# Hybrid state-space, pooling and stick-breaking block on one core: ScalarE empties the value products a pair at a time, output projection in 512-column blocks, other banks and earlier token sums ahead of the first seven-product block

## The chip, the cores and the metric

The kernel runs on one core of a Trainium2 chip. The metric is the device time of one launch in microseconds (us). PE is TensorE, with PEld its weight loads; DVE is VectorE, ACT is ScalarE, POOL is GpSimd, SP is SyncE, which here issues DMAs. The core has an SBUF of 128 partitions, in which tiles live, and a PSUM of eight banks, each 128 partitions x 512 fp32 columns, into which PE writes.

## The reference

One layer, sequence S = 1024, width D = 1024, all in float32. The heart of it is:

```python
h = rms_norm(x, norm_w)
z, xbc, dt_raw, pool_u, pool_gate, qkv, sb_gate, merge = split(h @ w_in)
y_ssm  = mamba2_branch(z, xbc, dt_raw, ...) @ w_proj_ssm     # causal conv, chunked scan, gate, norm
y_pool = pool_branch(pool_u, pool_gate, ...) @ w_proj_pool   # trailing means over 2, 4, 8, 16
y_sb   = stick_breaking_branch(qkv, sb_gate) @ w_proj_sb     # below
g = sigmoid(merge)                                           # three gates per channel
merged = g0 * y_ssm + g1 * y_pool + g2 * y_sb
return rms_norm(x + merged @ w_out, final_norm_w)
```

The attention has 16 heads of 64 and no softmax. For query t and key s < t, with z = q·k/8, its weight is sigmoid(z_s) times the product of sigmoid(−z) over the keys between s and t; a scan from the right computes that product. The result o = att @ v is multiplied by silu(gate).

## The kernel before

**Numbers.** Each fp32 operand is held as two fp32r parts, hi and lo, and a product is three matmuls, hi·hi, hi·lo and lo·hi. A contraction over 1024 is so 8 k-tiles x 3 = 24 matmuls into one bank. `gemm_b` (L396) has weights stationary and 512 tokens moving, `gemm_a` (L405) tokens stationary and 256 weight columns moving. Weights come in halves of 512 KB: `load_half` (L102) issues the DMA on SP, `split_half` (L110) makes hi on ACT (L128) and lo on DVE (L129) in a ring `wpool` of four halves; `mm()` (L413) hands out a PSUM bank in a fixed rotation, two of the pool `mm` and then `mmx` of the pool `mmx`, counted from `mmb`, and triggers the split of a coming half.

**Stages in the order of the program.**

1. `norm_in` (L548): eight tiles of x, row norms (Square on ACT L567, rsqrt on POOL L545, scale on DVE L573), transposes on PE (L588) into `hT` as hi (ACT) and lo (DVE L592). Constants: `cm` (identity, masks) and `cols` (per-channel vectors).
2. `conv_part` (L705): projection block x0 with its causal convolution, the last z block together with dt (`zd_open` L594 casts its weights, L605 and L606), gate block g0, x1, g1. Between them a table of steps puts the token sums `one`, `two`, `three` (L227 to L255): sums and differences of blocks of `hT`, each cast to hi on ACT (L260) and lo on DVE (L261).
3. Fourteen seven-product blocks (`seven_block` L281). A block of 256 columns x 1024 tokens is done with seven half-size products instead of eight, in four banks x, y, z, v. `seven_prep` (L140) makes the weight sums of a block, s1 to s4 and the hi and lo parts (`lo` is L176), for the first one inside g1's loop; the products are L299, the additions on DVE L309.
4. `attention_part` (L860): 64 units (p, hd, ip): eight pairs of heads, the head of the pair, and four groups of 256 queries. For each unit `stage_qk` (two scores' rows: matmuls L891, sigmoids on ACT L895 and L898, scan on DVE L900, multiplication L901 to `be`), `stage_tr` (transposes on PE L918, hi on ACT L920, lo on DVE L921) and `stage_av` (value products L942). The value products of a unit stand three sub-steps behind its transposes, so the last of them come in the loop of the next unit but one. Between the sub-steps PE is filled with projections for later (`fill`). All value products go to one bank `avs`, columns 0 to 255 for even ip, 256 to 511 for odd; the stationary v carries its hi part in 64 columns and its lo part in the other 64, so the bank's two 64-row halves hold two partial results, and a unit's end adds them: ACT copies one half out (L947), DVE adds the other from PSUM (L948). After an odd ip POOL multiplies by the gate (L950) and SP stores.
5. `ssd_part` (L1104), `pool_part` (L987).
6. `merge_part` (L1279): the three branches' projections and the gates, then the output projection: four blocks of 256 columns x eight token tiles, each 24 matmuls; DVE adds the residual (L1342), ACT squares with a row sum (L1344); in the last block each tile is finished one tile late: sum (L1329), rsqrt on POOL, a multiplication by r and the final weight (L1333), store (L1334).

**What sets the order.** PE's order is written by hand in the whole program; that of DVE, ACT and POOL too in `norm_in` and `conv_part` with the seven-product blocks. In attention and merge a scheduler orders ACT, POOL and DVE by estimated times, but for DVE in the output projection, which is again as written. Each engine then runs its list in order. SP issues DMAs in its list's order.

Of the kernel before, what the change touches and what calls it, by code (L numbers as in the profile page):

```python
# [8 lines left out]
F32 = mybir.dt.float32  # L9
# [34 lines left out]
def block_plan():  # L44
# [30 lines left out]
    for i in range(4):  # L75
        plan.append((("out", i), "w_out", 0, [(256 * i, 256)]))
    return plan
# [6 lines left out]
class Builder:  # L84
# [25 lines left out]
    def split_half(self):  # L110
        nc = self.nc
        n = self.wnext
        if n >= self.limit():
            return
        self.wnext += 1
        raw = self.raw.pop(n)
        if n // 2 == BLK["z", 0]:
            w = self.zd[:, :, 4 * (n % 2) : 4 * (n % 2) + 4, 0:256]
        else:
            w = self.wpool.tile([P, 2, 4, 256], F32R, tag="w", name=f"w{n}")  # L120
        raw = raw.rearrange("p (a b) -> p a b", b=256)
# [426 lines left out]
    def norm_in(self, pool, pps):  # L548

        nc = self.nc  # L550
        xts = []
        for t in range(8):
            xt = pool.tile([P, D], F32, tag="xt", name=f"xt{t}", bufs=8)
            nc.sync.dma_start(out=xt, in_=self.ins["x"][t * P : t * P + P, :])
            xts.append(xt)
            if t == 3:
                consts = self.constants()
                next(consts)
                self.load_half()
# [146 lines left out]
    def conv_part(self):  # L706
        with ExitStack() as ctx:
            ctx.enter_context(self.tc.manual_schedule(engines={mybir.EngineType.PE, mybir.EngineType.DVE, mybir.EngineType.Pool, mybir.EngineType.Activation}))
            pool = self.c_pool = self.sb(ctx, "c_sb", 3, "right")
            plain = ExitStack()  # L710
            self.ps_extra(plain, "c_ps", 3)
            pps = self.ps(plain, "n_ps", 3)

# [11 lines left out]
            for i, _ in enumerate(self.conv_gen(0, pool, norm)):  # L725
                if i == 2:
                    self.zd_open(dpool)
# [3 lines left out]
            one, two, three = self.seven_operands(tpool, dpool)  # L731
            dt = self.dt_part(dpool, {1: (one, 0), 3: (two, 0), 5: (one, 1), 7: (two, 1)})
            next(dt)
            zctx.close()
            self.tt[4] = self.sb(ctx, "t4_sb", 1, "right").tile([P, 2, 4, 512], F32R, name="tt4")
            steps = {8: (three, 0), 24: (three, 1), 48: (one, 2), 72: (three, 2)}
            for i, _ in enumerate(self.g_gen(0)):
# [7 lines left out]
            self.wseven = {}  # L745
            steps = {4: (two, 2), 16: (one, 3), 32: (three, 3), 44: (two, 3)}
            prep = {}
            for i, _ in enumerate(self.g_gen(1)):
                if i in steps:
                    steps[i][0](steps[i][1])  # L750
                if i == 14:
                    self.drain(dt)
                    dctx.close()
                    self.wspool = self.sb(ctx, "ws_sb", 2)
                if i == 50:
                    self.t_flush()
# [99 lines left out]
    def attention_part(self):  # L856
        tc, nc = self.tc, self.nc
        A, V, T, G = nc.scalar, nc.vector, nc.tensor, nc.gpsimd
        with ExitStack() as ctx:
# [64 lines left out]
            def stage_av(u, jc):  # L924
# [19 lines left out]
                if jc == ip:  # L944
                    other = slice(64 - 64 * hd, 128 - 64 * hd)
                    cs = slice(256 * (ip % 2), 256 * (ip % 2) + 256)
                    A.copy(o[rows, cs], ps[other])  # L947
                    V.tensor_tensor(out=o[rows, cs], in0=o[rows, cs], in1=ps[rows], op=ALU.add)  # L948
                    if ip % 2 == 1:
                        G.tensor_tensor(out=o[rows], in0=o[rows], in1=gt[rows], op=ALU.mult)  # L950
                        nc.sync.dma_start(out=self.d_y["sb"][p // 4][rows, p % 4, hs], in_=o[rows])

# [328 lines left out]
    def merge_part(self):  # L1281
        tc, nc = self.tc, self.nc
        A, V, T, G = nc.scalar, nc.vector, nc.tensor, nc.gpsimd
        with ExitStack() as ctx:
            ctx.enter_context(self.bigctx)
            self.ps_extra(ctx, "m_ps", 4)
            with ExitStack() as c2:
                pacc = self.sb(c2, "m_acc", 1, "right")
# [27 lines left out]
            with ExitStack() as c2:  # L1316
# [5 lines left out]
                for t in range(8):  # L1322
                    nc.sync.dma_start(out=res[t], in_=self.ins["x"][t * P : t * P + P, :])
                c2.enter_context(tc.manual_schedule(engines={mybir.EngineType.DVE}))

                def finish(t):
                    ot = pool.tile([P, D], F32, tag="ot", name="ot", bufs=3)
                    ss = pool.tile([P, 1], F32, tag="fss", name="fss", bufs=2)
                    V.tensor_reduce(out=ss, in_=ssq[:, t], axis=mybir.AxisListType.X, op=ALU.add)  # L1329
                    r = self.rstd(pool, ss, D, "f")  # L1330
                    step = D if t < 7 else D // 2
                    for c in range(0, D, step):
                        V.scalar_tensor_tensor(ot[:, c : c + step], res[t][:, c : c + step], r, fw[:, c : c + step], op0=ALU.mult, op1=ALU.mult)  # L1333
                        nc.sync.dma_start(out=self.out[t * P : t * P + P, c : c + step], in_=ot[:, c : c + step])  # L1334

                for b in range(4):
                    w = self.block(("out", b))
                    cs = slice(b * 256, b * 256 + 256)
                    for t in range(8):
                        ps = self.mm()[:, 0:256]  # L1340
                        self.drain(self.gemm_a(ps, w, lambda pt, k, t0, t1: mh[k][:, pt, t0:t1], t))
                        V.tensor_tensor(out=res[t][:, cs], in0=ps, in1=res[t][:, cs], op=ALU.add)  # L1342
                        sq = pool.tile([P, 256], F32, tag="sq", name="sq", bufs=2)
                        A.activation(sq, res[t][:, cs], AF.Square, accum_out=ssq[:, t, b : b + 1])  # L1344
                        if b == 3 and t > 0:
                            finish(t - 1)
                finish(7)


def host_arrays(i):  # L1350
# [7 lines left out]
    for _, src, row, cols in PLAN:  # L1358
        m = np.concatenate([mats[src][row : row + 1024, c : c + n] for c, n in cols], axis=1)
        blocks.append(tiles(m).reshape(P, 2048))  # L1360
# [43 lines left out]
```

## Time and profile before

| quantity | value |
|---|---|
| median of 3 runs | 2077.47 us (2076.37 to 2077.67) |
| the profiled execution, its own time | 2076.43 us |
| its span, first to last instruction | 2074.7 us |
| mean granted PE clock | 0.991 |
| busy: PE, PEld, DVE, ACT, POOL | 98%, 83%, 64%, 46%, 14% of the span |
| chain of work that ended last | PE 78%, DVE 15%, ACT 4% |
| stages | norm, convolution 0 to 155 us; seven-product blocks to 435; attention to 1200; scan, pooling to 1640; merge to 1974; output to 2074.7 |

The chain of the page follows the work that ended last back through what released it; the stage borders are read from the lines of PE's timeline and rounded. PE's list of waits tells, for each kind of instruction, what released it and for how long PE stood idle before.

### The profile page before, as it was taken

The page shows a single profiled execution, that of the slowest core. Times are in us where ns is not written, and L with a number is a line of the kernel's source. Part 1 is how long each engine was busy: PE and PEld are TensorE (multiplying, and loading weights), DVE is VectorE, ACT ScalarE, POOL GpSimd, SP SyncE. Part 2 cuts the span into 40 slices and gives each one's busy share as a digit, 9 for nine tenths or more (in the row PEclk, how much of TensorE's full clock was granted, in tenths as well). Part 3 has the DMA queues.
Part 4 walks back from the last instruction along what each step waited for, and adds up shares of the span by engine and source line. Part 5 has one row for each costly group of instructions (what it writes and reads, how often), then busy time and mean ns, then how long its engine had stood idle before and what let it go on. Part 6 is the DMA issues. An engine that isn't in the chain of part 4 may idle for free.

```text
span 2074.7 us, 29592 instructions
## 1 busy us (share of the span) xinstructions
PE 2026.5 (98%) x11312; PEld 1726.4 (83%) x11312; DVE 1333.1 (64%) x1857; ACT 952.4 (46%) x1953; POOL 292.5 (14%) x412
## 2 busy tenths in 40 slices
PE   8989999999999899999999899999999999999998
PEld 6978878788898788989898888778888788888898
DVE  6687788847767767676668647777657724424333
ACT  4353433335555655455556456667543423323231
POOL 3000000001111111010111124444200002221000
PEclk9999999999999999999999999999999999999999
DMA  5222232341121122112121266666464625433232
GB/s 201 94 95 102 85 119 91 112 155 57 42 72 36 41 78 61 57 56 68 55 72 46 62 201 210 198 201 200 140 202 142 213 92 192 144 115 107 82 132 82
DMA packets 116157, 234.00 MB, mean 113 GB/s; under 512 B 9776, under 2 KB 59696, under 8 KB 116016
## 3 DMA queue, kind: packets, MB, share of 16 engines
q1 hardware_dynamic: 116016, 232.12, 34.4%
q8 instruction: 89, 1.46, 0.3%
q14 instruction: 52, 0.43, 0.1%
HBM read 168.38 MB, written 63.70 MB: 112 GB/s over the span
## 4 chain that ended last, share of the span: by engine, by line
PE 78%; DVE 15%; ACT 4%; issue 3%; DMA 1%; DVEq 0%; POOL 0%; ACTq 0%; SPq 0%; POOLq 0%
PE mm L396 27%; PE mmx L396 14%; PE mm L405 12%; PE mmx L299 4%; DVE om L900 4%; PE mmx L405 4%; PE av L942 3%; DVE acc L358 3%; PE yd L1171 3%; PE tr L918 2%; PE mm L299 1%; PE yo L1174 1%; PE st L1177 1%; DVE be L901 1%; PE z L891 1%
## 5 line engine op out<-in xcount | busy, mean ns | idle before, releaser
L396 PE MATMUL mm<-hT,w 128*128 128x512 f32 x2232 | 584.3, 405 | 1.9 <-DVE hT L592 1.8
L396 PEld LDWEIGHTS mm<-hT,w 128*128 128x128 f32 x2232 | 406.2, 190 | 92.9 <-issue 15.1
L405 PE MATMUL mm<-w,hT 128*128 128x256 f32 x2112 | 287.9, 286 | 2.0 <-issue 1.1
L405 PEld LDWEIGHTS mm<-w,hT 128*128 128x128 f32 x2112 | 265.1, 191 | 3.4 <-ACT qb L835 1.6
L396 PE MATMUL mmx<-x,w 128*128 128x512 f32 x1008 | 230.3, 389 | 0.0
L129 DVE TENSOR_TENSOR w<-raw,w 128x1024 fp32r<-128x1024 f32 x116 | 150.1, 1296 | 113.3 <-ACT w L128 113.2
L396 PEld LDWEIGHTS mmx<-x,w 128*128 128x128 f32 x1008 | 189.3, 188 | 39.2
L900 DVE TENSOR_TENSOR_SCAN om<-om,zero 128x128 f32<-128x128 f32 (+7 forms) x128 | 175.5, 1372 | 61.8 <-ACT om L895 60.9
L920 ACT CAST attT<-tr 128x512 fp32r<-128x512 f32 (+2 forms) x224 | 98.3, 439 | 138.9 <-PE tr L918 86.1
L921 DVE TENSOR_TENSOR attT<-tr,attT 128x512 fp32r<-128x512 f32 (+2 forms) x224 | 111.2, 497 | 67.3 <-ACT attT L920 65.6
L128 ACT CAST w<-raw 128x1024 fp32r<-128x1024 f32 x116 | 121.5, 1050 | 61.2 <-PE mmx L396 27.6
L895 ACT ACTIVATE om<-z 128x128 f32<-128x128 f32 (+2 forms) x192 | 92.7, 496 | 68.0 <-PE z L894 67.1
L396 PE MATMUL mm<-x,w 128*128 128x512 f32 x528 | 122.6, 389 | 0.0
L1300 ACT ACTIVATE gt<-gt 128x1024 f32<-128x1024 f32 x32 | 34.0, 1062 | 185.9 <-DMA gt<-d_gate 185.9
L396 PEld LDWEIGHTS mm<-x,w 128*128 128x128 f32 x528 | 99.1, 188 | 20.6
L396 PE MATMUL mmx<-hT,w 128*128 128x512 f32 x456 | 105.0, 390 | 0.0
L901 DVE TENSOR_TENSOR be<-be,om 128x128 f32<-128x128 f32 (+7 forms) x128 | 98.1, 767 | 10.5
L396 PEld LDWEIGHTS mmx<-hT,w 128*128 128x128 f32 x456 | 85.4, 188 | 17.6
L1148 POOL TENSOR_TENSOR E<-E,cbm 128x1024 f32<-128x1024 f32 x32 | 76.6, 2395 | 160.9 <-issue 104.8
L898 ACT ACTIVATE be<-z 128x128 f32<-128x128 f32 (+2 forms) x192 | 92.5, 500 | 0.1
L918 PE MATMUL tr<-cm,be 128*128 128x128 f32 x576 | 90.3, 274 | 0.5 <-DVE be L901 0.5
L1309 POOL TENSOR_TENSOR acc<-acc,gt 128x512 f32<-128x512 f32 x32 | 45.6, 1426 | 247.0 <-DVE gt L1308 125.9
(250 smaller groups left out, 3255.7 us busy)
## 6 DMA issues: line engine op xcount, KB each, us to landing
raw<-in_wblk SPq DMA_DIRECT2D x148, 512.0 KB, 4.1
E<-d_act SPq DMA_DIRECT2D x32, 512.0 KB, 4.7
gt<-d_gate SPq DMA_DIRECT2D x32, 512.0 KB, 4.0
d_gate<-mg SPq DMA_DIRECT2D x16, 512.0 KB, 3.1
xi<-d_x SPq DMA_DIRECT2D x32, 256.0 KB, 3.2
zs<-d_z SPq DMA_DIRECT2D x32, 256.0 KB, 2.9
d_ssm<-yt SPq DMA_DIRECT2D x32, 256.0 KB, 3.1
xraw<-d_ssm SPq DMA_DIRECT2D x16, 512.0 KB, 6.0
```

Of the source, the lines that this page charges most:

```text
L128: nc.scalar.copy(hi, raw)
L129: nc.vector.tensor_tensor(out=lo, in0=raw, in1=hi.bitcast(F32), op=ALU.subtract)
L299: T.matmul(ps, w[a](i, k), mov[b](j, k), start=first and n == 0, stop=n == 11, skip_group_check=not first)
L396: T.matmul(ps, w(a, k, ct * P, ct * P + P), mov(b, k, half * 512, half * 512 + 512), start=n == 0, stop=n == 23)
L405: T.matmul(ps, sta(a, k, tok * P, tok * P + P), w(b, k, 0, ncol), start=n == 0, stop=n == 23)
L895: A.activation(om[:, c0 : c0 + n], z[:, 0:n], AF.Sigmoid, scale=-0.125)
L898: A.activation(be[:, c0 : c0 + n], z[:, 0:n], AF.Sigmoid, scale=0.125)
L900: V.tensor_tensor_scan(out=rev, data0=rev, data1=self.zero.broadcast_to((P, L)), initial=1.0, op0=ALU.mult, op1=ALU.add)
L901: V.tensor_tensor(out=be[:, 0:L], in0=be[:, 0:L], in1=om[:, 1 : L + 1], op=ALU.mult)
L918: T.transpose(tr[:, c : c + P], b[:, (2 * jc + j) * P : (2 * jc + j + 1) * P], self.ident)
L920: A.copy(at[:, 0, sl], tr[:, sl])
L921: V.tensor_tensor(out=at[:, 1, sl], in0=tr[:, sl], in1=at[:, 0, sl].bitcast(F32), op=ALU.subtract)
```

## The change

Six edits:

- **Value products (L934 on).** The bank is a fresh tile per pair of units (pool `a_av`, one buffer). Only after the odd ip it is emptied: ACT copies all of it to SBUF (`oa`), ACT copies the other head half across to `o`, DVE adds the two from SBUF over 512 columns; multiplication and store as before.
- **Output projection.** Two blocks of 512 columns, each of four halves (two k-tiles x 512 columns), 24 matmuls of 512 columns per token tile; the host lays `w_out` out accordingly. Halves 0, 1, 6 and 7 go to a pool of their own, the triggers by `mm()` are off. The last tile's second block is done in two pieces of 256 columns, its columns multiplied by the final weight ahead of the norm, and at the end DVE scales one half and ACT the other.
- **First seven-product block.** The pool of the norm's banks is opened before the convolution's, and the rotation starts two later (`mmb -= 2`), so a block takes `mmx` four times and the next `mmx` twice and `mm` twice.
- **Token sums.** `one`, `two`, `three` come earlier in the loops of dt, g0 and g1, as do the six steps of the first block's weight sums.
- **Constants.** `cm` and `cols` load after x tile 0 instead of x tile 3.
- **dt.** `zd_open` comes after the second instead of the third step of the first convolution's loop.

```diff
-    for i in range(4):
-        plan.append((("out", i), "w_out", 0, [(256 * i, 256)]))
+    for i in range(4):
+        plan.append((("out", i), "w_out", 512 * (i % 2), [(512 * (i // 2), 512)]))
...
+        elif n - 2 * BLK["out", 0] in (0, 1, 6, 7):
+            w = self.wext.tile([P, 2, 4, 256], F32R, tag="wx", name=f"w{n}")
...
+        consts = self.constants()
         for t in range(8):
+            if t == 1:
+                next(consts)
...
             if t == 3:
-                consts = self.constants()
-                next(consts)
...
+            pps = self.ps(plain, "n_ps", 3)
             self.ps_extra(plain, "c_ps", 3)
-            pps = self.ps(plain, "n_ps", 3)
...
-                if i == 2:
+                if i == 1:
                     self.zd_open(dpool)
...
-            dt = self.dt_part(dpool, {1: (one, 0), 3: (two, 0), 5: (one, 1), 7: (two, 1)})
+            dt = self.dt_part(dpool, {0: (one, 0), 2: (two, 0), 4: (one, 1), 6: (two, 1)})
-            steps = {8: (three, 0), 24: (three, 1), 48: (one, 2), 72: (three, 2)}
+            steps = {2: (three, 0), 18: (three, 1), 36: (one, 2), 60: (three, 2), 84: (two, 2)}
...
-            steps = {4: (two, 2), 16: (one, 3), 32: (three, 3), 44: (two, 3)}
+            steps = {2: (one, 3), 20: (three, 3), 34: (two, 3)}
...
-                if i == 50:
+                if i == 46:
                     self.t_flush()
                     prep = self.seven_prep(BLK[SEVEN[0]])
-                if i > 50 and i % 8 == 0 and prep:
+                if i % 8 == 6 and prep:
                     prep.pop(min(prep))()
...
             self.ps_extra(ctx, "seven_ps", 6)
+            self.mmb -= 2
...
-            avs = self.ps(ctx, "a_av", 1).tile([P, 512], F32, name="av")
+            pav = self.ps(ctx, "a_av", 1)
...
+                    if ip % 2 == 0:
+                        av[0] = pav.tile([P, 512], F32, tag="av", name="av")
-                ps = avs[:, 256 * (ip % 2) : 256 * (ip % 2) + 256]
+                ps = av[0][:, 256 * (ip % 2) : 256 * (ip % 2) + 256]
...
-                if jc == ip:
+                if jc == ip and ip % 2 == 1:
                     other = slice(64 - 64 * hd, 128 - 64 * hd)
-                    cs = slice(256 * (ip % 2), 256 * (ip % 2) + 256)
-                    A.copy(o[rows, cs], ps[other])
-                    V.tensor_tensor(out=o[rows, cs], in0=o[rows, cs], in1=ps[rows], op=ALU.add)
-                    if ip % 2 == 1:
-                        G.tensor_tensor(out=o[rows], in0=o[rows], in1=gt[rows], op=ALU.mult)
+                    oa = pool.tile([P, 512], F32, tag="oa", name="oa", bufs=1)
+                    A.copy(oa, av[0])
+                    A.copy(o[rows], oa[other])
+                    V.tensor_tensor(out=o[rows], in0=o[rows], in1=oa[rows], op=ALU.add)
+                    G.tensor_tensor(out=o[rows], in0=o[rows], in1=gt[rows], op=ALU.mult)
...
-                for b in range(4):
-                    w = self.block(("out", b))
-                    cs = slice(b * 256, b * 256 + 256)
+                def piece(d, t, c0, c1, n):
+                    ps = self.mm()[:, 0 : c1 - c0]
+                    w = lambda part, k, a, b: wd[k // 2][:, part].rearrange("p a b -> p (a b)")[:, 512 * (k % 2) + c0 - 512 * d + a : 512 * (k % 2) + c0 - 512 * d + b]
+                    self.drain(self.gemm_a(ps, w, lambda pt, k, t0, t1: mh[k][:, pt, t0:t1], t, c1 - c0))
+                    r = res[t][:, c0:c1]
+                    V.tensor_tensor(out=r, in0=ps, in1=r, op=ALU.add)
+                    sq = pool.tile([P, 512], F32, tag="sq", name="sq", bufs=2)[:, 0 : c1 - c0]
+                    A.activation(sq, r, AF.Square, accum_out=ssq[:, t, n : n + 1])
+                    if t == 7:
+                        V.tensor_tensor(out=last[:, c0:c1], in0=r, in1=fw[:, c0:c1], op=ALU.mult)
+                for d in range(2):
+                    while self.wnext < first + 4 * d + 4:
+                        self.split_half()
+                    wd = [self.wh.pop(first + 4 * d + i) for i in range(4)]
                     for t in range(8):
-                        ps = self.mm()[:, 0:256]
...
-                        if b == 3 and t > 0:
-                            finish(t - 1)
-                finish(7)
+                        if (d, t) != (1, 7):
+                            piece(d, t, 512 * d, 512 * d + 512, d)
+                        if d == 0 and t in (2, 4):
+                            self.split_half()
+                        if d == 1 and t > 0:
+                            root(t - 1)
+                            if t < 7:
+                                finish(t - 1)
+                piece(1, 7, 512, 768, 1)
...
+                finish(6)
+                piece(1, 7, 768, 1024, 2)
...
+                V.tensor_scalar(last[:, 0:512], last[:, 0:512], r, None, op0=ALU.mult)
+                nc.sync.dma_start(out=self.out[7 * P :, 0:512], in_=last[:, 0:512])
+                A.activation(last[:, 512:D], last[:, 512:D], AF.Copy, scale=r)
+                nc.sync.dma_start(out=self.out[7 * P :, 512:D], in_=last[:, 512:D])
```

Line numbers of the new kernel are two higher from L128 on, four higher in attention and up to seven higher at the end of the value products.

DVE's list where the first pair of units ends its value products (other pairs have the like), before (`om` is the scan, `be` the multiplication, `attT` the lo part of the transposed weights, `o` the add of a unit's end, `va`, `vb` and `zsg` a projection's):

```order
459 L901 TENSOR_TENSOR be<-be,om 128x896
460 L921 TENSOR_TENSOR attT<-tr,attT 128x512
461 L900 SCALAR_TENSOR_TENSOR om<-om,zero 128x1024
462 L948 TENSOR_TENSOR o<-o,av 64x256
463 L901 TENSOR_TENSOR be<-be,om 128x1024
464 L921 TENSOR_TENSOR attT<-tr,attT 128x512
465 L803 TENSOR_TENSOR va_3638<-mm,va_3638 128x2x64
466 L805 TENSOR_TENSOR vb_3639<-mm,vb_3639 128x2x64
467 L921 TENSOR_TENSOR attT<-tr,attT 128x256
468 L808 TENSOR_TENSOR zsg<-zsg,mm 128x256
469 L921 TENSOR_TENSOR attT<-tr,attT 128x128
470 L948 TENSOR_TENSOR o<-o,av 64x256
```

and in the changed kernel at the same place:

```order
459 L905 TENSOR_TENSOR be<-be,om 128x896
460 L925 TENSOR_TENSOR attT<-tr,attT 128x512
461 L904 SCALAR_TENSOR_TENSOR om<-om,zero 128x1024
462 L905 TENSOR_TENSOR be<-be,om 128x1024
463 L925 TENSOR_TENSOR attT<-tr,attT 128x512
464 L807 TENSOR_TENSOR va_3637<-mm,va_3637 128x2x64
465 L809 TENSOR_TENSOR vb_3638<-mm,vb_3638 128x2x64
466 L925 TENSOR_TENSOR attT<-tr,attT 128x256
467 L812 TENSOR_TENSOR zsg<-zsg,mm 128x256
468 L925 TENSOR_TENSOR attT<-tr,attT 128x128
469 L955 TENSOR_TENSOR o<-o,oa 64x512
470 L904 SCALAR_TENSOR_TENSOR om<-om,zero 128x128
```

The first unit's add, which stood behind the 1024-column scan, is gone, and one add of 512 columns from SBUF stands where the second unit's add was, one row earlier.

DVE's list at the end of g1, ahead of the first seven-product block, before (`gsg` is the gate's multiplication from PSUM, `tt` the lo part of a token sum, `s` the weight sums, `w` and `ws` the lo parts of weights, of which the first is that of a11):

```order
152 L787 TENSOR_TENSOR gsg<-gsg,mmx 128x512
153 L261 TENSOR_TENSOR tt_525<-td,tt_525 128x512
154 L179 TENSOR_TENSOR s_1238<-raw_970,raw_1059 128x512
155 L180 TENSOR_TENSOR s_1239<-s_1238,raw_970 128x512
156 L183 TENSOR_TENSOR s_1240<-raw_970 128x512
157 L184 TENSOR_TENSOR s_1241<-raw_1059,s_1239 128x512
158 L787 TENSOR_TENSOR gsg<-gsg,mm 128x512
159 L176 TENSOR_TENSOR w_1235<-raw_970,w_1235 128x4x128
160 L176 TENSOR_TENSOR ws_1237<-raw_1059,ws_1237 128x4x256
161 L176 TENSOR_TENSOR w_1235<-s_1239,w_1235 128x4x128
```

and in the changed kernel:

```order
151 L247 TENSOR_TENSOR td<-td,te 128x512
152 L263 TENSOR_TENSOR tt_525<-td,tt_525 128x512
153 L181 TENSOR_TENSOR s_1229<-raw_977,raw_1066 128x512
154 L182 TENSOR_TENSOR s_1230<-s_1229,raw_977 128x512
155 L791 TENSOR_TENSOR gsg<-gsg,mmx 128x512
156 L185 TENSOR_TENSOR s_1231<-raw_977 128x512
157 L186 TENSOR_TENSOR s_1232<-raw_1066,s_1230 128x512
158 L178 TENSOR_TENSOR w_1226<-raw_977,w_1226 128x4x128
159 L178 TENSOR_TENSOR ws_1228<-raw_1066,ws_1228 128x4x256
160 L791 TENSOR_TENSOR gsg<-gsg,mm 128x512
```

Behind the weight sums only one multiplication from PSUM, of an `mmx` bank, is left ahead of a11's lo part; the last two, of `mm` banks, stand behind it.

PE's list where the last seven-product block gives way to attention's first projection, before:

```order
553 L299 MATMUL mmx<-hT_107,ws_2974 128x512 x3
554 L299 MATMUL mmx<-hT_108,ws_2974 128x512 x3
555 L299 MATMUL mmx<-hT_109,ws_2974 128x512 x3
556 L299 MATMUL mmx<-hT_110,ws_2974 128x512 x3
557 L299 MATMUL mmx<-tt_818,ws_2974 128x512 x12
558 L299 MATMUL mmx<-hT_107,ws_2974 128x512 x3
559 L299 MATMUL mmx<-hT_108,ws_2974 128x512 x3
560 L299 MATMUL mmx<-hT_109,ws_2974 128x512 x3
561 L299 MATMUL mmx<-hT_110,ws_2974 128x512 x3
562 L405 MATMUL mm<-w_3139,hT_103 128x256 x3
```

and in the changed kernel:

```order
553 L301 MATMUL mmx<-hT_107,ws_2974 128x512 x3
554 L301 MATMUL mmx<-hT_108,ws_2974 128x512 x3
555 L301 MATMUL mmx<-hT_109,ws_2974 128x512 x3
556 L301 MATMUL mmx<-hT_110,ws_2974 128x512 x3
557 L301 MATMUL mm<-tt_818,ws_2974 128x512 x12
558 L301 MATMUL mm<-hT_107,ws_2974 128x512 x3
559 L301 MATMUL mm<-hT_108,ws_2974 128x512 x3
560 L301 MATMUL mm<-hT_109,ws_2974 128x512 x3
561 L301 MATMUL mm<-hT_110,ws_2974 128x512 x3
562 L407 MATMUL mm<-w_3139,hT_103 128x256 x3
```

The last products go to banks of the pool `mm` instead of `mmx`, and the projection that follows takes a bank of `mm` as before.

## Rows read from the trace of the kernel before

**Rows 1.** The profile's page, part 1: busy us (share of the span), instructions.

```profile
PE 2026.5 (98%) x11312; PEld 1726.4 (83%) x11312; DVE 1333.1 (64%) x1857; ACT 952.4 (46%) x1953; POOL 292.5 (14%) x412
```

**Rows 2.** The waits of PE, whole run: us in total, times, longest.

```profile
PE av L942 <- DVE o L948: 18.3, 14, 3.0
PE mm L299 <- DVE gsg L787: 5.3, 1, 5.3
PE tp L588 <- DMA cm<-in_cmat: 2.2, 1, 2.2
...
PE mmx L405 <- DVE zd L605: 1.7, 1, 1.7
```

**Rows 3.** One stretch of the run (attention): length, busy us of each engine, PEclk, DMA, GB/s.

```profile
435.00:1200.00 765.00, 742.38 (x4913) 661.70 (x4912) 529.40 (x758) 412.08 (x935) 98.42 (x253) 0.99 0.19 57
```

**Rows 4.** Timeline, 537.2 to 541.2 us: start, duration, engine, operation [idle before it].

```profile
537.91 2.28 DVE L900 TENSOR_TENSOR_SCAN om<-om,zero 128x1024 f32<-128x1024 f32 x1
538.05 0.36 ACT L947 COPY o<-av 64x256 f32<-64x256 f32 x1
...
540.22 0.42 DVE L948 TENSOR_TENSOR o<-o,av 64x256 f32<-64x256 f32 x1
...
540.70 0.80 PE L942 MATMUL av<-attT,vb 128*128 128x256 f32 x2 [2.64 <-DVE o L948]
```

**Rows 5.** Windows, PE alone: length, busy us, granted clock.

```profile
540.46:543.87 3.41, 3.17 (x10) 0.50 0.00 0
...
1182.15:1185.60 3.45, 3.21 (x16) 0.51 0.00 0
144.50:151.30 6.80, 3.64 (x9) 0.50 0.47 156
```

**Rows 6.** Timeline at a pair's end, 547.2 to 549.8 us.

```profile
547.23 0.36 ACT L947 COPY o<-av 64x256 f32<-64x256 f32 x1
...
549.74 0.36 PE L942 MATMUL av<-attT,vb 128*128 128x256 f32 x1
```

**Rows 7.** ACT by line and shape: busy us, mean ns, idle before.

```profile
L1078 ACT COPY mg<-mm 128x512 f32<-128x512 f32 x48 | 27.9, 582 | 41.8 <-PE mm L396 41.7
...
L947 ACT COPY o<-av 64x256 f32<-64x256 f32 x64 | 23.5, 368 | 22.5 <-PE av L942 18.0 <-issue 3.5
```

**Rows 8.** Timeline of the first seven-product block, 141.5 to 148.4 us.

```profile
146.92 0.68 DVE L787 TENSOR_TENSOR gsg<-gsg,mm 128x512 f32<-128x512 f32 x1
...
147.52 0.68 DVE L176 TENSOR_TENSOR w<-raw,w 128x512 fp32r<-128x512 f32 x1
```

**Rows 9.** Timeline at the start of attention, 421 to 437 us.

```profile
424.79 11.67 PE L405 MATMUL mm<-w,hT 128*128 128x256 f32 x96
...
426.63 0.68 DVE L309 TENSOR_TENSOR cx<-mmx,pu 128x512 f32<-128x512 f32 x1
```

**Rows 10.** Timeline of PE in 512- and 256-column streams: start, duration, count.

```profile
1952.29 11.04 PE L396 MATMUL mm<-x,w 128*128 128x512 f32 x48
...
1963.17 11.04 PE L396 MATMUL mmx<-x,w 128*128 128x512 f32 x48
...
2014.36 5.92 PE L405 MATMUL mm<-w,mg 128*128 128x256 f32 x48
...
2031.64 5.92 PE L405 MATMUL mm<-w,mg 128*128 128x256 f32 x48
```

**Rows 11.** Timeline of the end, 2065.9 us on.

```profile
2066.40 0.42 DVE L1342 TENSOR_TENSOR res<-mmx,res 128x256 f32<-128x256 f32 x1 [0.18 <-PE mmx L405]
...
2067.80 1.28 DVE L1333 SCALAR_TENSOR_TENSOR ot<-res,r,fw 128x1024 f32<-128x1024 f32 x1 [0.73 <-POOL r L545]
...
2070.07 1.42 DVE L1333 SCALAR_TENSOR_TENSOR ot<-res,r,fw 128x512 f32<-128x512 f32 x2 [0.73 <-POOL r L545]
```

**Rows 12.** Timeline of the start, 3 to 11 us.

```profile
5.70 1.06 ACT L567 ACTIVATE sq<-xt 128x1024 f32<-128x1024 f32 x1 [0.20 <-DMA xt<-in_x]
...
7.39 1.06 ACT L567 ACTIVATE sq<-xt 128x1024 f32<-128x1024 f32 x1 [0.55 <-DMA xt<-in_x]
```

More of the change, by code (lines that the diff above doesn't have):

```diff
@@ L943, in stage_av @@
                         n += 1
-                if jc == ip:
+                if jc == ip and ip % 2 == 1:
                     other = slice(64 - 64 * hd, 128 - 64 * hd)
-                    cs = slice(256 * (ip % 2), 256 * (ip % 2) + 256)
-                    A.copy(o[rows, cs], ps[other])
-                    V.tensor_tensor(out=o[rows, cs], in0=o[rows, cs], in1=ps[rows], op=ALU.add)
-                    if ip % 2 == 1:
-                        G.tensor_tensor(out=o[rows], in0=o[rows], in1=gt[rows], op=ALU.mult)
-                        nc.sync.dma_start(out=self.d_y["sb"][p // 4][rows, p % 4, hs], in_=o[rows])
+                    oa = pool.tile([P, 512], F32, tag="oa", name="oa", bufs=1)
[3 more added lines that the diff above has]
+                    G.tensor_tensor(out=o[rows], in0=o[rows], in1=gt[rows], op=ALU.mult)
+                    nc.sync.dma_start(out=self.d_y["sb"][p // 4][rows, p % 4, hs], in_=o[rows])
             n = len(units)
@@ L1286, in merge_part @@
             self.ps_extra(ctx, "m_ps", 4)
+            self.wext = self.sb(ctx, "o_w", 2)
             with ExitStack() as c2:
@@ L1324, in merge_part @@
                 c2.enter_context(tc.manual_schedule(engines={mybir.EngineType.DVE}))
-                def finish(t):
[L1327 to L1334, printed above, removed]
@@ L1336, in merge_part @@
-                for b in range(4):
-                    w = self.block(("out", b))
-                    cs = slice(b * 256, b * 256 + 256)
-                    for t in range(8):
-                        ps = self.mm()[:, 0:256]
[L1341 to L1344, printed above, removed]
-                        if b == 3 and t > 0:
-                            finish(t - 1)
@@ L1347, in merge_part, with root @@
-                finish(7)
+                self.due = None
+                first = 2 * BLK["out", 0]
+                roots = {}
+                def root(t):
+                    ss = pool.tile([P, 1], F32, tag="fss", name="fss", bufs=2)
+                    V.tensor_reduce(out=ss, in_=ssq[:, t, 0:2], axis=mybir.AxisListType.X, op=ALU.add)
+                    roots[t] = self.rstd(pool, ss, D, "f")
+                def finish(t):
+                    ot = pool.tile([P, D], F32, tag="ot", name="ot", bufs=2)
+                    V.scalar_tensor_tensor(ot, res[t], roots.pop(t), fw, op0=ALU.mult, op1=ALU.mult)
+                    nc.sync.dma_start(out=self.out[t * P : t * P + P, :], in_=ot)
@@ new lines, in merge_part @@
+                last = pool.tile([P, D], F32, name="last")
+                base = pool.tile([P, 1], F32, name="base")
+                def piece(d, t, c0, c1, n):
[8 more added lines that the diff above has]
+                        V.tensor_tensor(out=last[:, c0:c1], in0=r, in1=fw[:, c0:c1], op=ALU.mult)
@@ new lines, in merge_part @@
+                piece(1, 7, 512, 768, 1)
+                s = pool.tile([P, 1], F32, name="s7")
+                V.tensor_reduce(out=s, in_=ssq[:, 7, 0:2], axis=mybir.AxisListType.X, op=ALU.add)
+                V.tensor_scalar(base, s, 1.0 / D, EPS, op0=ALU.mult, op1=ALU.add)
+                finish(6)
+                piece(1, 7, 768, 1024, 2)
+                ms = pool.tile([P, 1], F32, name="ms7")
+                V.tensor_scalar(ms, ssq[:, 7, 2:3], 1.0 / D, base, op0=ALU.mult, op1=ALU.add)
@@ L1350, in host_arrays @@
+                r = pool.tile([P, 1], F32, name="r7")
+                G.tensor_tensor(out=r, in0=ms, in1=self.m05, op=ALU.pow)
+                V.tensor_scalar(last[:, 0:512], last[:, 0:512], r, None, op0=ALU.mult)
+                nc.sync.dma_start(out=self.out[7 * P :, 0:512], in_=last[:, 0:512])
+                A.activation(last[:, 512:D], last[:, 512:D], AF.Copy, scale=r)
+                nc.sync.dma_start(out=self.out[7 * P :, 512:D], in_=last[:, 512:D])
 def host_arrays(i):
@@ L1358, in host_arrays @@
     for _, src, row, cols in PLAN:
-        m = np.concatenate([mats[src][row : row + 1024, c : c + n] for c, n in cols], axis=1)
+        height = P * 2048 // sum(n for _, n in cols)
+        m = np.concatenate([mats[src][row : row + height, c : c + n] for c, n in cols], axis=1)
         blocks.append(tiles(m).reshape(P, 2048))
```

## The prediction, made before the changed kernel was run

> **What bounds the kernel now.** I read the page's part 1 first: TensorE (PE) is busy for 2026.5 of a span of 2074.7 us [rows 1], so the time is PE's work plus what PE waits for, and a change helps if it shortens a PE instruction, takes away a PE wait, or shortens the two ends. Next the waits of PE alone [rows 2]. One releaser stands out: the value products of attention wait 18.3 us in 14 places for VectorE's (DVE) add L948; the other waits are single ones at a stage's border. Attention is 765 us long with PE busy for 742.4, DVE for 529.4 and ACT for 412.1 [rows 3], so only PE is near its limit there. The timeline shows how the wait arises [rows 4]. `avs` is one bank of PSUM for both units of a pair. Unit 0's value products end while the planned order already has unit 3's sigmoids running; ACT copies at 538.05, but DVE's add stands behind the 1024-column scan that began at 537.91 and lasted 2.28, so it runs at 540.22, and PE's next value product, in the other half of the bank, comes at 540.70 after 2.64 us idle. Then the clock: at four of the long waits the granted clock afterwards is 0.50 to 0.51, the lower of the two levels, for about 3.4 us [rows 5], whose first two rows are the first and the last of the four, though PE was busy in nearly all of it; the first of them begins in the very wait of [rows 4].
>
> **Attention.** Each pair of units now gets the bank as one tile, and only the pair's end empties it, with one ACT copy of 128x512. Inside a pair nothing is read from the bank any more, so what the add L948 holds up there goes: −18.3. The four slow stretches have no cause left: in each PE was busy for about 3.3 of 3.4 us at half speed, which is half of 13.2 lost, −6.6. What replaces the wait stands at a pair's end. There [rows 6] the copy started at 547.23 and PE's next product came at 549.74, 2.51 later; a 128x512 copy from PSUM takes 582 ns on ACT where the small one took 368 [rows 7], so the bank is free at 547.81, 1.9 us early. DVE's add reads SBUF from now on and no longer holds the bank. ACT gains 2 x 0.59 − 2 x 0.37 = 0.44 us per pair, 14 us in 765, on an engine with 353 idle [rows 3]; DVE loses 32 adds. What is next when PE comes up to 25 us earlier over the stage is the chain of the next unit: sigmoids, scan, multiplication, transposes, cast, subtraction, on ACT and DVE, both with idle time. I put 2.0 on new short waits there, a little less than one wait like that of [rows 4]. Bounds: 0 if the lead holds everywhere; 12.5, half of the gain, if it is used up at the wide units. Sum −18.3 − 6.6 + 2.0 = −22.9.
>
> **dt.** PE waits 1.7 us for the cast L605 [rows 2], which was queued on DVE behind the convolution's last multiplications. Opened one step earlier it is out of the way: −1.7 (0 to −1.9).
>
> **First seven-product block.** Before, product 1 goes into an `mm` bank that DVE's L787 still reads: PE waits 5.3 us [rows 2], until 146.92 + 0.68 [rows 8]; the clock is then at 0.50 until 151.3, with 3.64 busy, 1.8 lost [rows 5]. Together 7.1 can go. Now the block starts with `mmx` banks that have been free for long. But the next thing late is known: the low part of a11 (L176) began only at 147.52 [rows 8], and the third matmul of the product needs it; were DVE's queue the same, nothing would be gained. It is shorter: one token sum (four DVE instructions over 128x512, 0.68 each as in [rows 8], 2.7) has left this stretch. One L787 also stands behind L176 now instead of ahead of it, which I leave out, since L176 may then wait for ACT's cast. That brings L176 about 2.7 earlier against the rest, and the earlier dt and the later start move all of it by 1.3. Of the 5.3 plus the 0.5 from 147.66 to L176's end at 148.20 some 3 stays as a wait in the product's first matmuls, and about half of the 1.8: −3.5, between 0 and −7.1.
>
> **Start of attention.** The same shift makes the last seven-product block take its last two banks from `mm`, of which the next stage's first projection needs one at once. Before it began at 424.79, while DVE's last-but-one add L309 ran at 426.63 [rows 9]; now it has to wait for an add of that place: 426.63 + 0.68 − 424.79 = 2.5. I take +2.0, as DVE may come to that add somewhat sooner than PE does; bounds 0 and 4.1 (2.5, and 1.6 for one stretch at the lower clock, as in [rows 5]).
>
> **Output projection.** 32 pieces of 24 matmuls with 256 columns become 15 with 512 and two with 256. In the trace 144 matmuls of 256 columns take 2031.64 − 2014.36 = 17.28, 0.120 each, and 48 of 512 take 1963.17 − 1952.29 = 10.88, 0.227 each [rows 10]. Before 768 x 0.120 = 92.2; after 360 x 0.227 + 48 x 0.120 = 87.5: −4.7. The Trainium skill speaks against this term: the page TensorE: Matmul & The Clock Gate, section Back-to-back issue gap, gives an isolated matmul N/2.4 + 2.5 ns, so that joining two halves would save only 2.5 ns, and by that the term would be some −1.0 (an estimate from the page). By it the whole would come to 2045.1 + 3.6 = 2048.7. The trace does not agree: its 256-column spacing is 0.120, not the page's 0.109. All four halves of a column block must be there at its start, and the second block's last two are cast and subtracted at the border: there DVE has the t = 7 add, the multiplication by `fw` (0.69 each by the add of 512 columns in [rows 9]) and the subtraction of about 1.2 ahead of matmul 14 of the next piece, 2.6 against 14 x 0.227 = 3.2. That just fits; +0.1. Sum −4.6, between 0 and −4.7.
>
> **Tail.** From the last add (2066.40) to the end of the span are 8.3 us [rows 11]: Square, then DVE's multiplication of token tile 6 (2067.80, 1.28) stands in front of the sum of tile 7, then two multiplications in 1.42 one behind the other. Now tile 6 is finished before the last piece, so the sum comes about 1.4 earlier, and the last 1024 columns are halves on two engines at once, 0.7 less: −2.1 (−0.8 to −2.8).
>
> **Start.** The constants, 194 KB together, now load ahead of x tiles 1 to 3. Two x tiles of 512 KB end 1.69 us apart, as far as their squares show, which wait for the DMA [rows 12]; 194/512 of it is 0.64 later. PE's own wait of 2.2 for `cm` [rows 2] isn't what sets the time, because later transposes need the scaled tiles, which hang on the squares; +0.4, between −0.8 and +0.7.
>
> **Sum.** −22.9 − 1.7 − 3.5 + 2.0 − 4.6 − 2.1 + 0.4 = −32.4. The profiled execution took 2076.43 (span 2074.7 and 1.7 around it), so 2044.0; the median of the runs is 1.04 above it: 2045.1.
>
> **Rivals.** (A) The forecast, chance 0.72, own range 2037 to 2053.
> (B) The waits move rather than go: with PE earlier, the transposes or the value products wait for DVE in the wide units, where scans of 2.28 and multiplications stand in a row. For it: DVE was 69% busy over the stage and the shown add was late by a scan. Against it: PE's whole idle time there, 765 − 742.4 = 22.6, is little more than the one wait's 18.3 [rows 2, 3], so transposes and scores have hardly waited so far. Half of 24.9 lost instead of 2.0 makes 10.5 more: 2055.6. Chance 0.13.
> (C) Slower than before: ACT, now alone in freeing the bank, takes its copy behind sigmoids and casts, so PE waits at the 31 pair ends after the first. It decides when it costs 32.4/31 = 1.05 us at each, that is if the copy is 1.9 + 1.05, about 3 us, later than in [rows 6]; at 1.5 us each it gives 2045.1 + 46.5 = 2091.6. Against it: ACT has idle time and its copy follows the last product at once. Chance 0.03.
> (D) The waits go, but the clock and the first block give nothing: PE may pause elsewhere instead. 6.6 + 3.5 back: 2055.2. Chance 0.07.
> (E) Nothing new is late: the first block gains all of 7.1, no new waits in attention or at its start: 3.6 + 2.0 + 2.0 better, 2037.5. Chance 0.05.
>
> **How the numbers follow.** 0.2%, about 4.2 us, is what a measurement of this kernel can tell from no change. A, B, D and E are all below 2073.3, and only C and some unforeseen mishap are not: faster 0.93, same 0.03, slower 0.04. Range 2036 to 2057, which takes in B, D and E and leaves out C and the outer parts of the bounds.
>
> **What would show it right or wrong.** In the profile after, the wait of the value products should be gone from PE's list or name ACT's copy with less than 3 us in all; attention should be about 23 us shorter with no stretch at the lower clock in it; the first block should wait for L178 (the old L176) for 2 to 4 us; a new wait of 2 to 3 us should stand ahead of the first projection of attention; the output stage should be 4 to 5 us shorter, the end 6.2 us. A wait of the transposes for the multiplication `be` of over 8 us speaks for B; a value wait on ACT at most of the pair ends speaks for C. I am wrong if attention is shorter by less than 12 us.

## The result, and the profile after

The changed kernel took 2047.08 us (median of 4 runs, 2046.28 to 2048.35) against 2077.53 before in the same comparison, a ratio of 0.9855 (95% interval 0.9838 to 0.9872). The forecast was 2045.1. The profiled execution has a span of 2045.6 after 2074.7, so 29.1 less where 32.4 were forecast.

The table cuts both traces at the same instructions of PE: the second projection matmul, the first dt matmul, the first matmul of product 2 of the first seven-product block, attention's first projection, the scan stage's first matmul (L1135, now L1141), the output projection's first and its last matmul's end.

| stretch of PE's timeline | before | after | difference | forecast |
|---|---|---|---|---|
| start to second projection matmul | 16.18 | 17.47 | +1.3 | +0.4 |
| to dt | 33.51 | 31.05 | −2.5 | −1.7 |
| to product 2 of the first block | 102.53 | 96.80 | −5.7 | −3.5 |
| to attention's first projection | 272.57 | 276.69 | +4.1 | +2.0 |
| to the scan stage | 787.10 | 767.57 | −19.5 | −22.9 |
| to the output projection | 762.16 | 762.25 | +0.1 | 0 |
| output projection | 92.31 | 87.54 | −4.8 | −4.6 |
| its end to the span's end | 8.3 | 6.2 | −2.1 | −2.1 |

PE's waits in attention after (430 to 1185 us; in total, times, longest), which answer to the first of [rows 2]:

```profile
PE mm L398 <- ACT qb L839: 2.4, 3, 1.2
PE mm L407 <- ACT qb L839: 2.0, 2, 1.5
PE tr L922 <- DVE attT L925: 1.6, 4, 0.8
PE tr L922 <- DVE be L905: 1.4, 3, 0.9
PE z L895 <- ACT be L902: 1.2, 1, 1.2
PE av L948 <- ACT oa L953: 1.1, 2, 0.6
```

The 18.3 us are gone; the value products wait 1.1 us in all, for ACT. At the place of [rows 4] the scan is as long as before, and PE's next value product (536.70) waits for nothing:

```profile
534.01 2.29 DVE L904 TENSOR_TENSOR_SCAN om<-om,zero 128x1024 f32<-128x1024 f32 x1
...
536.70 0.64 PE L948 MATMUL av<-attT,vb 128*128 128x256 f32 x4
...
541.08 0.59 ACT L953 COPY oa<-av 128x512 f32<-128x512 f32 x1
...
541.71 0.50 PE L948 MATMUL av<-attT,vb 128*128 128x256 f32 x2 [0.58 <-ACT oa L953]
```

The last two rows are one of the two pair ends that do cost something: PE follows the copy. The clock, in windows as [rows 5], is at the lower level in one stretch of attention only, and at full speed in the first block:

```profile
423.30:426.75 3.45, 3.45 (x19) 0.51 0.84 251
140.50:146.00 5.50, 3.77 (x17) 1.00 0.59 194
```

The first block, as [rows 8]:

```profile
140.57 0.61 PE L301 MATMUL mmx<-hT,w 128*128 128x512 f32 x2
...
142.18 0.68 DVE L178 TENSOR_TENSOR w<-raw,w 128x512 fp32r<-128x512 f32 x1
...
142.91 2.57 PE L301 MATMUL mmx<-hT,w 128*128 128x512 f32 x10 [1.73 <-DVE w L178]
```

Product 1 starts at once in a free bank and waits at its third matmul for a11's low part, which comes 5.3 us earlier than before. The start of attention, as [rows 9]:

```profile
415.73 0.69 DVE L311 TENSOR_TENSOR cx<-mm,cx 128x512 f32<-128x512 f32 x1 [3.58 <-DMA d_bc<-cx]
...
416.48 3.01 PE L301 MATMUL mm<-hT,ws 128*128 128x512 f32 x12 [1.54 <-DVE cx L311]
...
421.19 0.68 DVE L311 TENSOR_TENSOR cx<-mm,pu 128x512 f32<-128x512 f32 x1
...
422.01 2.71 PE L407 MATMUL mm<-w,hT 128*128 128x256 f32 x16 [2.52 <-DVE cx L311]
```

There are two waits for DVE's additions, the second the forecast one, and the slow clock of 423.3 comes behind them. The end, as [rows 11]:

```profile
2039.41 0.42 DVE L1355 TENSOR_TENSOR res<-mmx,res 128x256 f32<-128x256 f32 x1
...
2040.76 0.55 POOL L1383 TENSOR_TENSOR r<-ms,m 128x1 f32<-128x1 f32 x1 [3.20 <-DVE ms L1381]
2041.34 0.72 ACT L1386 ACTIVATE last<-last,r 128x512 f32<-128x512 f32 x1 [0.91 <-POOL r L1383]
2041.34 0.49 DVE L1384 TENSOR_SCALAR last<-last,r 128x512 f32<-128x512 f32 x1 [0.66 <-POOL r L1383]
```

### The profile page after: what moved, and what is told of

Same layout as the page of the kernel before. It is cut to its first block, busy times and chain, and to the rows that moved or that the text cites. A ratio compares the mean times of both kernels' runs of the same rounds, so it can differ in the third digit from the quotient of the medians.

```text
span 2045.6 us, 28762 instructions
## 1 busy us (share of the span) xinstructions
PE 2013.4 (98%) x10952; PEld 1702.1 (83%) x10952; DVE 1336.4 (65%) x1813; ACT 958.0 (47%) x1924; POOL 293.4 (14%) x412
## 4 chain that ended last, share of the span: by engine, by line
PE 77%; DVE 14%; ACT 4%; issue 3%; DMA 1%; SPq 0%; POOL 0%; DVEq 0%; POOLq 0%; ACTq 0%
PE mm L398 25%; PE mmx L398 15%; PE mm L407 13%; PE mmx L301 5%; PE mmx L407 3%; DVE om L904 3%; PE av L948 3%; DVE acc L360 3%; PE yd L1177 3%; PE tr L922 2%; DVE be L905 2%; PE mm L301 1%; PE yo L1180 1%; PE st L1183 1%; PE z L895 1%
## 5 line engine op out<-in xcount | busy, mean ns | idle before, releaser
L904 DVE TENSOR_TENSOR_SCAN om<-om,zero 128x128 f32<-128x128 f32 (+7 forms) x128 | 183.3, 1433 | 52.0 <-ACT om L899 51.0
```

Of the source, the lines that this page charges most:

```text
L904: V.tensor_tensor_scan(out=rev, data0=rev, data1=self.zero.broadcast_to((P, L)), initial=1.0, op0=ALU.mult, op1=ALU.add)
```

## The experiments

The stretches of the table, in us, for every run (the code ahead of attention is that of the changed kernel in pair_dve, unit_act, av_undone and pool_copy, and that of the kernel before in av_alone and before_again; `all three` joins the edits of mmb4, consts_undone and pool_copy):

| run | median | to 2nd matmul | to dt | dt to attention | attention | out | end |
|---|---|---|---|---|---|---|---|
| before | 2077.53 | 16.18 | 33.51 | 375.10 | 787.10 | 92.31 | 8.3 |
| after | 2047.08 | 17.47 | 31.05 | 373.49 | 767.57 | 87.54 | 6.2 |
| av_alone | 2059.67 | 16.57 | 33.16 | 380.16 | 767.41 | 92.31 | 8.3 |
| pair_dve | 2050.49 | 18.87 | 30.93 | 373.47 | 770.78 | 87.54 | 6.2 |
| unit_act | 2046.43 | 18.46 | 31.54 | 373.52 | 765.12 | 87.52 | 6.2 |
| av_undone | 2068.90 | 17.65 | 31.57 | 373.02 | 788.54 | 87.53 | 6.2 |
| mmb4 | 2045.06 | 18.17 | 30.95 | 370.72 | 767.39 | 87.53 | 6.2 |
| banks_undone | 2048.53 | 18.07 | 31.40 | 375.97 | 767.42 | 87.53 | 6.2 |
| sums_undone | 2052.88 | 17.54 | 31.89 | 379.19 | 767.58 | 87.54 | 6.2 |
| consts_undone | 2046.83 | 16.39 | 31.90 | 373.95 | 767.36 | 87.54 | 6.2 |
| pool_copy | 2044.76 | 17.92 | 31.55 | 373.92 | 763.73 | 87.54 | 6.2 |
| all three | 2042.27 | 16.86 | 31.98 | 370.83 | 764.86 | 87.53 | 6.2 |
| before_again | 2081.95 | 16.79 | 33.21 | 380.10 | 787.32 | 92.31 | 8.3 |

The runs were measured in three comparisons, in which the kernel before took 2079.85 (av_alone to av_undone), 2078.67 (mmb4 to consts_undone) and 2080.23 (the others), against 2077.53 beside the result. Medians of different comparisons that are 2 or 3 apart therefore show little by themselves; the stretches say more. The edits of the output projection, of the tail and of `zd_open` were not run by themselves: for them there are the stretches alone.

**The value products alone, and all but them.** The kernel before with the edit of the value products, and the changed kernel without it.

> The kernel before with the new value products alone (bank per pair, emptied by ACT, add from SBUF). Theory: the attention stage loses the wait of 18.3 us on DVE's add and the four slow stretches and gains 3 to 5 us of new short waits, so 20 to 22 us off the kernel before, 2055.5 to 2057.5; the last transposes of attention come 20 to 22 us earlier against the start of the stage. Rival: part of the stage's gain comes from the other edits (banks at its start, an earlier start), then less than 15 us, over 2062.

> The changed kernel with the value products as before. Theory: the attention stage gets 20 to 22 us longer, 2067 to 2069, with the wait on DVE's add at about 18 us and slow stretches again. Rival: the other edits shift the stage's start so that fewer adds meet a scan: under 2062.

Ratios to the kernel before 0.9906 (0.9891 to 0.9920) and 0.9948 (0.9933 to 0.9963). The edit alone gives attention −19.7, without a stretch at the lower clock in it; taking it out gives +21.0, with five such stretches, 20.5 us together, and the old wait back to a tenth:

```profile
PE av L946 <- DVE o L952: 18.2, 14, 3.0
```

So attention's gain is this edit's. The first median missed its range by 2, though it is 20.2 below the kernel before of its own comparison. The excess isn't in attention: the stretch from dt to attention took 5.1 more than in the first profile of before, with the same code. That was asked of the kernel before itself:

> The kernel before, once more with a profile, for the stretch from the dt projection to the first projection of attention, which took 375.1 us in its first profile and 380.2 with the same code in the run with the value products alone. Theory (the stretch varies by some us from run to run with the clock and with DMA in it): 375 to 381. Rival: 375.1 within 0.5, and the value products cost something there.

It took 380.1. Two stretches at the lower clock lie in it that the first profile has not (length, busy us, granted clock); PE was busy throughout them, and half of 6.8, so 3.4, was lost:

```profile
51.20:54.60 3.40, 3.40 (x16) 0.50 0.20 80
426.65:430.05 3.40, 3.40 (x9) 0.50 0.41 159
```

And PE stands behind an add that waits for a store to have read its tile, for 2.06 us where the first profile had 0.34 (the first two rows; the others are those of the second):

```profile
421.18 0.69 DVE L309 TENSOR_TENSOR cx<-mmx,cx 128x512 f32<-128x512 f32 x1 [2.38 <-DMA d_bc<-cx]
...
421.92 3.03 PE L299 MATMUL mmx<-hT,ws 128*128 128x512 f32 x12 [0.34 <-DVE cx L309]
```

```profile
424.92 0.69 DVE L309 TENSOR_TENSOR cx<-mmx,cx 128x512 f32<-128x512 f32 x1 [4.10 <-DMA d_bc<-cx]
...
425.67 4.60 PE L299 MATMUL mmx<-hT,ws 128*128 128x512 f32 x12 [2.06 <-DVE cx L309]
```

**Who empties the bank, and when.** In pair_dve the pair stays, DVE reads PSUM; in unit_act each unit empties its half, by ACT.

```diff
-                    A.copy(oa, av[0])
-                    A.copy(o[rows], oa[other])
-                    V.tensor_tensor(out=o[rows], in0=o[rows], in1=oa[rows], op=ALU.add)
+                    A.copy(o[rows], av[0][other])
+                    V.tensor_tensor(out=o[rows], in0=o[rows], in1=av[0][rows], op=ALU.add)
```

> The changed kernel, but at a pair's end ACT copies only the other 64 rows and DVE adds the rest straight from PSUM over 512 columns, as before. Theory: when the bank is read (only at a pair's end, where PE comes back 2.5 us later) is what counts, not who reads it: within 3 us of the changed kernel, 2044 to 2050, with a value wait on DVE of under 5 us. Rival: it matters that DVE no longer holds the bank; the add stands behind a scan at pair ends too, and 10 us or more come back, over 2057.

```diff
+                if jc == ip:
+                    oa = pool.tile([P, 256], F32, tag="oa", name="oa", bufs=2)
+                    A.copy(oa, ps)
+                    A.copy(o[rows, cs], oa[other])
+                    V.tensor_tensor(out=o[rows, cs], in0=o[rows, cs], in1=oa[rows], op=ALU.add)
```

> The changed kernel with the bank emptied at each unit's end again (two halves), but by an ACT copy of 128x256 and an add from SBUF. Theory by the bank's reader: inside a pair PE then waits for ACT's copy alone, 0.4 to 0.6 us in each of 32 places, no slow clock: 8 to 15 us in waits at most, 2050 to 2060. Rival (the reading inside the pair itself is what costs, whoever does it): the wait returns with 15 to 20 us and slow stretches, 2065 to 2072.

0.9858 (0.9842 to 0.9875) and 0.9840 (0.9825 to 0.9854). PE's value waits, first pair_dve, then unit_act:

```profile
PE av L948 <- DVE o L953: 8.0, 5, 2.8
```

```profile
PE av L946 <- ACT oa L952: 1.3, 2, 0.8
```

With DVE reading at pair ends alone 8.0 us of waits remain, and attention takes 770.78, still 17.8 less than in av_undone. With ACT reading inside the pair too 1.3 us remain, and attention takes 765.12, 2.4 less than in the changed kernel, of which up to 1.7 is that the slow clock fell ahead of attention there. So either half of the edit brings most of the gain without the other: to empty the bank only at the pair's end, or to let ACT instead of DVE read it. Under DVE the pair is worth 17.8; under ACT these runs show no worth of it. For pair_dve both the theory ("when, not who": a wait under 5 us) and its rival (10 us or more back) missed: 8.0 us and 3.2 more in attention lie between them. For unit_act the theory was too dear, with 8 to 15 us of waits and 2050 or more, and the rival fell.

**Banks and sums.** The first run starts the rotation four later (`mmb -= 4`), the second has the old order of the pools and the old rotation, the third the old steps of the token and weight sums.

> The changed kernel with the rotation of banks started four later instead of two (mmb -= 4): a seven-product block takes mmx four times, the next mm twice and then mmx twice, so the last block ends on mmx banks and attention's first projection takes a bank whose last reader is an early ACT copy. Theory (the new wait at attention's start is that of the mm bank for DVE's add): the wait of 2.5 us and the slow clock of some 1.7 us behind it go, 2042 to 2044. Rival (DVE is late there anyway, and the wait moves to the next instruction that needs it): under 1 us off, 2046 to 2048.

> The changed kernel with the old order of bank pools and the old rotation; token sums stay early. Theory: product 1 waits again for an mm bank's multiplication by the gate, which now stands behind a11's low part, so the first block starts 3 to 4 us later with 1 to 2 us of slow clock; attention's start gets its 2.5 and 1.7 us back: 2045.5 to 2049 in sum, with the two visible apart in the trace. Rival (the bank was never what held product 1, a11's low part was): the first block is as fast as in the changed kernel and the sum is 2042 to 2044.

> The changed kernel with token sums and weight sums at their old places; the banks stay changed. Theory: a11's low part is then late by about 4 us and product 1 waits for it, with slow clock behind: 4 to 6 us slower than the changed kernel, 2051 to 2053. Rival (the free bank alone brings the gain): within 1.5 us of the changed kernel.

0.9840 (0.9823 to 0.9856), 0.9858 (0.9844 to 0.9873) and 0.9877 (0.9862 to 0.9892). PE in banks_undone, then sums_undone:

```profile
145.61 5.49 PE L301 MATMUL mm<-hT,w 128*128 128x512 f32 x12 [3.91 <-DVE gsg L790]
```

```profile
147.51 2.08 PE L301 MATMUL mmx<-hT,w 128*128 128x512 f32 x4 [3.81 <-DVE w L178]
```

Either half alone leaves a wait of 3.8 to 3.9 and a slow clock in the block. The bank is worth 2.5 from dt to attention (4.6 at the block, of which 2.1 is given back up to attention's start), the sums 5.7. In mmb4 the wait of 2.5 is gone and the slow clock with it, 2.8 from dt to attention, but attention is only 0.2 shorter. PE's busy time in it (the second number; first the changed kernel, then mmb4) falls by 1.3 with the slow stretch. Its idle time rises from 9.9 to 11.1, as a wait that the changed kernel had lost is back:

```profile
422.01:1189.58 767.57, 757.64 (x5048) 1.00 0.22 63
419.84:1187.23 767.39, 756.33 (x5049) 1.00 0.21 64
```

```profile
PE mm L407 <- issue: 1.1, 1, 1.1
```

So the medians differ by 2.0 and the two stretches together by 3.0, where 4.2 was hoped for; 2045.06 lies between the ranges of the theory and its rival.

**Constants.**

> The changed kernel with the constants loaded after x tile 3 again. Theory (x tiles 1 to 3 land later because of the constants, and the norm's chain hangs on them): the second projection matmul starts 1.0 to 1.5 us earlier and the whole is that much shorter, 2045.5 to 2046.2. Rival (PE needs the constants first, as its wait for cm in the kernel before said): 0 to 2 us longer.

Ratio 0.9847 (0.9832 to 0.9861). The second matmul came at 16.39, at 16.18 to 16.86 in the other four with this order, and 17.47 to 18.87 in the eight with the new one. In the medians 0.25 is no difference, and 2046.83 lies outside the range, so the price is shown at the start and not in the whole. The squares of x tile 1 show it, first consts_undone, then the changed kernel, against 5.70 in [rows 12]:

```profile
5.64 1.06 ACT L569 ACTIVATE sq<-xt 128x1024 f32<-128x1024 f32 x1 [0.19 <-DMA xt<-in_x]
```

```profile
7.48 1.06 ACT L570 ACTIVATE sq<-xt 128x1024 f32<-128x1024 f32 x1 [1.73 <-DMA xt<-in_x]
```

**ACT's share, and a better version.** `G.tensor_copy(o[rows], oa[other])` instead of `A.copy`; then this with mmb4 and consts_undone.

> The changed kernel with the second copy of a pair's end (from oa to the other 64 rows) on POOL instead of ACT. Theory (ACT's extra 0.4 us per pair makes it late for the casts L839 that PE waits for): those waits fall from 4.4 to about 1 us as in the run in which ACT copied 64 rows only, attention gets 2 to 4 us shorter, 2043 to 2045. Rival: POOL's copy is longer, DVE's add stands waiting for it in its list and holds up scans behind it; waits of the transposes for DVE rise from 3.0 to over 6 us, 2047 or more.

> The changed kernel with three edits: rotation four later, constants after x tile 3, second copy on POOL. Theory: the gains add, 2.0 and 1.1 and 3, so 2040 to 2042.5, below both kernels. Rival (a wait that goes is taken up by the next, as half of the bank's gain was): 2043 to 2045.

0.9825 (0.9811 to 0.9840) and 0.9814 (0.9799 to 0.9829). PE's waits on `qb` fall from 4.4 to 3.4 only, those of the transposes from 3.0 to 1.5 (pool_copy):

```profile
PE mm L407 <- ACT qb L839: 2.0, 2, 1.5
PE mm L398 <- ACT qb L839: 1.4, 3, 0.9
PE tr L922 <- DVE be L905: 1.0, 3, 0.5
...
PE tr L922 <- DVE attT L925: 0.5, 2, 0.3
```

With all three edits attention is 2.5 shorter than in mmb4, both without a slow stretch in it. So much the copy on POOL saves, but not mainly through `qb` as the theory had it. All three edits give 2042.27, 4.8 below the changed kernel, measured in another comparison; the profiles' spans differ by 5.1.

## Why the prediction was right, and by how much its terms were off

- **Attention, −22.9, measured −19.5.** The mechanism holds: in the two runs that isolate the edit, the wait and the slow stretches go and come with it. Mis-sized is the term of 2.0 for new short waits; it measured 5.6. PE's busy time in the stage fell from 764.5 to 757.6, by 6.9 where I had 6.6, though one new slow stretch lies in it. Its idle time fell from 22.6 to 9.9, by 12.7 where I had 18.3 − 2.0 = 16.3. The list after shows where the 5.6 went: ACT's `qb` casts 4.4 after 0.8, the transposes' waits for DVE 3.0 after 0.5, ACT's copy 1.1 after none, while all other idle time shrank by 1.7 (rows of before: the stage, then two of PE's waits):

```profile
424.79:1211.89 787.10, 764.48 (x5049) 0.99 0.21 63
```

```profile
PE mm L405 <- ACT qb L835: 0.8, 1, 0.8
PE tr L918 <- DVE be L901: 0.5, 2, 0.3
```

  That ACT would do at pair ends was right; rival (C) had 1.1 us in place of 32. My reason, that the pair's end leaves time, holds for most of the gain (pair_dve), but unit_act shows that with ACT as reader the time isn't needed.
- **dt, −1.7, measured −2.5.** The wait for `zd` is gone from PE's list. In consts_undone, which starts as before, the stretch is 31.90, so −1.6; the other 0.9 goes with the later start of the changed kernel.
- **Start, +0.4, measured +1.3,** and up to 2.7 in the other profiles with this order. The term was mis-sized: the landing of x tile 1 slipped by 1.8, not 0.64, as the square's row shows. My sum had only the share of bytes. SP also issues its DMAs one behind the other, and tile 1's goes out at 2.12, behind two constants of 0.4 each (first three rows); before, four tiles went out from 0.74 on in 1.82 (last row). How the 1.8 divides between the two the runs don't show.

```profile
1.19 0.41 SPq L523 DMA_DIRECT2D cm<-in_cmat  x1
1.66 0.42 SPq L526 DMA_DIRECT2D cols<-in_cols  x1
2.12 1.38 SPq L559 DMA_DIRECT2D xt<-in_x  x3
```

```profile
0.74 1.82 SPq L554 DMA_DIRECT2D xt<-in_x  x4
```

- **First block, −3.5, measured −5.7.** a11's low part came at 142.18; I had about 143.5. The wait was 1.73 where I had 3, and the clock stayed up behind it, where I had half of a slow stretch.
- **Start of attention, +2.0, measured +4.1.** The wait is the forecast one, 2.52 where I worked out 2.5 and then took off 0.5, as DVE might come to the add sooner; it didn't. A further 1.2 is the add that waits for the store, 1.54 after 0.34, which I had not priced; it varies between 0.3 and 2.1.
- **Output and tail** came out as worked out, −4.8 and −2.1. The start-to-start spacing 0.227 holds for the new code: 48 matmuls in 1962.71 − 1951.83 = 10.88. By the rule for an isolated matmul in the Trainium skill's page TensorE: Matmul & The Clock Gate, section Back-to-back issue gap, it would have been some −1.0 (an estimate from the page). The trace doesn't agree: 92.31 − 87.54 is 4.8. That rule is for an isolated matmul and these stand in a stream, so it was no fair rival of this term.

```profile
1951.83 11.04 PE L407 MATMUL mmx<-w,mg 128*128 128x512 f32 x48
1962.71 11.04 PE L407 MATMUL mm<-w,mg 128*128 128x512 f32 x48
```

- Rivals (B), (D) and (E) failed: the transposes wait 3.0 in all, of the slow stretches one is left, in a new place, and new waits there are. That one stretch in attention was not forecast, and the first block's wait is just under the 2 to 4 us that were. The span's gain came within 3.3 of the forecast partly by luck, because errors of both signs met: three of the eight stretches were off by 2 or more.

## What to carry to other kernels

A bank that two engines must read comes free when the later of them gets to it in its own list: give the bank to the engine whose list has nothing long ahead, and let the other work from SBUF, or empty the bank where the writer comes back late. Here either brought most of the gain. Shifting a rotation of banks can move the wait to the block where the rotation meets the next stage; look at both ends. A single profile of a kernel may be one of its faster executions: before holding a stage's length against another kernel's, have a second one.

## What was not expected

The same code from dt to attention took 375.1 and 380.1 us in two executions of the kernel before. The two more stretches at the lower clock (3.4) and the longer wait for the store `d_bc` (DVE stood 4.10 instead of 2.38, PE 2.06 instead of 0.34) make up the difference. What starts the first of these stretches, right behind dt's wait of 1.7 us, in one execution and not in the other, the runs don't show. In the ten profiles in which dt is opened earlier and that wait is gone, no stretch at the lower clock lies between the one at the very start, which every profile has, and the first block; of the three with the wait two have one (before_again, av_alone). So the edit of dt may be worth up to 1.7 more than the table shows, against an execution that has that stretch. A fourth buffer for the tile that the store reads wasn't tried.
